# FF1 in a two-layer decoder step: eight pairs of output tiles per layer by seven block products instead of eight

## The chip, the cores and the metric

The kernel runs on one core of one Trainium2 chip. The metric is device time in microseconds (us). The profile names the engines PE (matmul), PEld (the weight loads of PE), DVE, ACT and POOL (elementwise work), and SP (a queue that issues DMAs). PE, DVE, ACT, POOL and SP each have an instruction stream of their own, taken in the order written, and meet at semaphores.

## The reference

Two layers over 512 prompt tokens and 8 sample tokens, model width 1024. What matters here is the feed-forward part, with hidden width 4096:

```python
u = x @ lp['w_in']
...                                   # attention, recurrence, pooling
mix = jnp.concatenate([attn, rec, pool], axis=-1) @ lp['w_out']
x = layer_norm(alpha * x + mix, lp['ln1_g'], lp['ln1_b'])
hid = jnp.square(jax.nn.relu(x @ lp['w_ff1']))                          # FF1: 1024 -> 4096
x = layer_norm(alpha * x + hid @ lp['w_ff2'], lp['ln2_g'], lp['ln2_b'])  # FF2: 4096 -> 1024
```

All data are float32.

## The kernel before

Activations lie transposed: 128 channels on the partitions, tokens along the free dimension, 8 such blocks for 1024 channels. Tokens come in two halves h: half 0 has 256 prompt tokens, half 1 has 256 prompt tokens and the 8 sample tokens, 264 in all (`NH`).

Each float32 operand is split into a high and a low part for PE: `xh` and `xl` for the layer's input x, `hh` and `hl` for the hidden activations, and the two planes of a weight slot. For a weight block w and an input block x three matmuls are issued: high by high, high by low, low by high. So a product of one 128-wide output tile with one token half takes 8 blocks x 3 = 24 matmuls (`product`), accumulated in one PSUM bank.

A weight tile of 128 output columns (a "unit") is split on its way: a DMA of 1 MB brings two units into one of two `raw` buffers, ACT (or POOL) casts the high plane into one of seven slots `w0` to `w6`, and DVE (or POOL) subtracts to get the low plane (`prep_to`).

The feed-forward part runs in 4 chunks p of 1024 hidden channels. For a chunk, `do_f1` makes the 8 output tiles of FF1 (ACT: relu out of PSUM into `ra`; DVE: square into `rb`; ACT: cast to `hh`; DVE: remainder to `hl`), and `do_f2` makes 8 products of FF2 whose results DVE adds to `y`. Half 0 runs chunk 0 alone, while the first layer norm of half 1 is still being computed; then both halves run chunks 1 to 3, half 0 leading by three units (`lagged`, `STEADY`); then half 1 runs chunk 0 again alone (called chunk 4), while the second norm of half 0 is computed.

The order on each engine is set at build time: every operation is recorded with its estimated duration, and a list scheduler (`Plan.order`) places them by due time. Where an operation has two possible engines (`copy`, `either`), the scheduler chooses. All instructions are issued from one line (`Plan.issue`), so the profile shows one line number for nearly everything, and one reads by tile names: `mm`, `s`, `t`, `x` are PSUM banks (3, 2, 2 and 1 of them), `acc`, `gq`, `ra`, `rb`, `rc`, `rd`, `gl` are temporaries of one token line, and `p` and `long` in the profile are wide temporaries of attention and norms.

Of the kernel before, what the change touches and what calls it, by code (L numbers as in the profile page):

```python
# [59 lines left out]
class Plan:  # L60
# [60 lines left out]
    def add(self, first, *others):  # L121

        op = Op()
        eng, method, args, kw = first
        outs = [kw[k] for k in ("out", "accum_out") if kw.get(k) is not None]
        rest = list(args)
        if "out" not in kw:
            outs.append(rest.pop(0))
        if method == "tensor_tensor_reduce":
            outs.append(rest.pop())  # L130
        ins = [a for a in rest if isinstance(a, bass.AP)]
        ins += [a for k, a in kw.items() if k not in ("out", "accum_out") and isinstance(a, bass.AP)]
        op.idx = len(self.ops)
        self.ops.append(op)
        op.alts, op.preload = {}, False
        for e, m, ar, k in others + (first,):
            op.eng, op.call = e, (getattr(self.engs[e], m), ar, k)
            self.cost(op, m, outs, ins, ar, k)
            op.alts[e] = (op.call, op.dur, op.sets, op.lock)
        deps = set()  # L140
        for a, w in [(a, False) for a in ins] + [(a, True) for a in outs]:
            nm = a.name
            if a.space == bass.MemoryType.DRAM:
                continue
            r = self.region(a)
            wl, rl = self.writes.setdefault(nm, []), self.reads.setdefault(nm, [])

            def hit(q):
                return q[0] < r[1] and r[0] < q[1] and any(x < d and c < y for x, y in q[2] for c, d in r[2])
            for q, o in wl:  # L150
                if hit(q):
                    deps.add(o)
            if w:
                for q, o in rl:
# [12 lines left out]
        deps.discard(op)  # L167
        op.deps = deps
        return op

    def cost(self, op, method, outs, ins, args, kw):
# [6 lines left out]
        op.lock = (op.eng == "G" and bool(ins) and method != "dma_start") or (op.eng == "V" and (  # L178
            len(sb) > 1 or (len(sb) == 1 and method in ("tensor_scalar", "tensor_copy"))))
        op.sets, op.bytes = None, 0  # L180
        op.side = op.eng == "T" and out.name[:2] != "mm"
        if method == "dma_start":
            b = 4
            for k in out.shape:
# [135 lines left out]
def trunk_kernel(ctx, tc, x_prompt, x_sample, cache_k, cache_v, state_h, state_conv, state_pool,  # L320
# [30 lines left out]

    def wide(name, long=False):

        return plan.tile(tmp, [128, 1056], F32, "long" if long else "p4", 1 if long else 2, name)

    def line(tag, width, name=None, parts=128, dt=F32):
        return plan.tile(tmp, [128, 288], dt, tag, 1, name or tag)[:parts, :width]

    def t_bank(shape, name="tb"):
# [85 lines left out]
    def prep_to(i):  # L445
        while nxt[0] <= min(i, len(units) - 1):
            j = nxt[0]
            nxt[0] += 1
            raw_need(j)
            key, _, view, s = units[j]  # L450
            src = view(raw_t[j], s)
# [58 lines left out]
    KZ = ctile([128, 2, 512], "KZ")  # L510
    G.memset(KZ[64:128, 0], 0.0)
    G.memset(KZ[0:64, 1], 0.0)
    onesm = ctile([128, 128], "onesm")
    G.memset(onesm, 1.0 / DM)
    epsc = ctile([128, 2], "epsc")
# [96 lines left out]


    y = {}
    xh = [act.tile([128, 8, NH[h]], F32R, tag="xh%d" % h, name="xh%d" % h) for h in range(2)]
    xl = [act.tile([128, 8, NH[h]], F32R, tag="xl%d" % h, name="xl%d" % h) for h in range(2)]
    hid = {}

    def new_hid(h):
# [2 lines left out]
    def load_x(h):  # L622
# [3 lines left out]
        for k4 in range(2):  # L626
            for t0, n, src in blocks:
# [49 lines left out]

    def layer_start(l):
        st.clear()
        load_gates(l)  # L680
# [3 lines left out]
        st["Q", 1] = plan.tile(tmp, [128, 4, NH[1]], F32, "Q1", 1, "Q1")  # L684
        st["V"] = plan.tile(tmp, [128, 4, 128], F32, "V", 1, "V")
# [6 lines left out]
        st["col"] = plan.tile(tmp, [128, 2, 43], F32, "col", 1, "colt")  # L692
# [211 lines left out]
    class Item:  # L904
# [34 lines left out]
        def turn(self):  # L939
            self.pts = []  # L940
            for b in range(self.nk // 128):
                pt = t_bank([128, 4, 128])
                for g in range(4):
                    T.transpose(pt[:, g], self.pr[:, g, b * 128:b * 128 + 128], ident)
                p = plan.tile(tmp, [128, 512], F32, "P", 4, "P")
                copy(p, pt.rearrange("p g n -> p (g n)"), "V")
                self.pts.append((b, p))

# [96 lines left out]
    class Norm:  # L1045
# [103 lines left out]
        def split(self):  # L1149
# [7 lines left out]
            for m in range(8):  # L1157
                hi, lo = xh[self.h][:, m], xl[self.h][:, m]
                z, b = self.sq[m % 2], self.col("b", m)
                V.scalar_tensor_tensor(z, yy[:, m], self.col("g", m), r, MUL, MUL)  # L1160
                if m % 2 == 0 or not MIXED:
# [112 lines left out]
    def do_f1(l, p, m, h):  # L1274
# [9 lines left out]
        S.copy(out=hi[:, m], in_=q)  # L1284
        V.tensor_tensor(lo[:, m], q, hi[:, m].bitcast(F32), SUB)

    def do_f2(l, p, m, h):
        ps = product((l, "f2%d" % p, m // 2, m % 2), h, hid[h][0], hid[h][1])
        if p == h:
            residual(h, m, ps)  # L1290
        else:
            V.tensor_tensor(y[h][:, m], y[h][:, m], ps, ADD)
        if p == 3 + h:
            norms[l, h, 2].chunk(m)

    def do_ff(l, kind, p, m, h):

        (do_f1 if kind == "f1" else do_f2)(l, p, m, h)

    def body():  # L1300
        layer_start(0)
# [3 lines left out]
        for l in range(DEPTH):  # L1305
# [67 lines left out]
                        stage(c)  # L1373
            drain()
            shift_states(l)
            both = [(kind, p, m) for p in range(1, 4) for kind in ("f1", "f2") for m in range(8)]
            ff = [((kind, 0, m), 0) for kind in ("f1", "f2") for m in range(8)]
            ff += lagged(both, STEADY, STEADY)
            ff += [((kind, 4, m), 1) for kind in ("f1", "f2") for m in range(8)]
            for (kind, p, m), h in ff:  # L1380
                prep_to(uidx[(l, "%s%d" % (kind, p), m // 2, m % 2)])
                if h == 1 and (kind, p, m) == both[0]:
                    drain()
                do_ff(l, kind, p, m, h)
                slot_end()
            drain()
# [33 lines left out]
```

## Time and profile before

| | |
|---|---|
| median of 3 runs | 1122.9 us (1122.36 to 1122.96) |
| the profiled execution's own time | 1121.61 us |
| its span | 1119.9 us |
| mean granted PE clock | 0.996 |
| DVE busy | 670.9 us |
| ACT busy | 525.4 us |
| POOL busy | 233.8 us |

The span is what the trace covers; 1.7 us of the execution's own time lie around it. The profiled execution was 1.3 us under the median. Busy shares are averages over stages with different limits, so the prediction reads the feed-forward stage by itself. A matmul's duration in the profile overlaps the next one's; the rate is read from many matmuls in a row.

### The profile page before, as it was taken

The numbers are of one execution on the slowest core, as the hardware profiler recorded it, in microseconds if no ns is written. First come the engines' busy times: TensorE is split into PE (matmuls) and PEld (weight loads), VectorE is DVE, ScalarE is ACT, GpSimd is POOL, SyncE is SP. The second block draws the span as 40 slices with busy tenths as digits, with TensorE's granted clock in tenths as the row PEclk, the third lists the DMA queues.
The fourth block names the chain that finished last, engine by engine and source line by source line (L and its number), as shares of the span: only waits on it lengthen the run. The fifth ranks groups of instructions, "written<-read, shape, count | busy, mean of one in ns | idle before, by whom it ended". The sixth has DMA issues, their size and how long they took to land.

```text
span 1119.9 us, 21316 instructions
## 1 busy us (share of the span) xinstructions
PE 1095.7 (98%) x8733; PEld 1068.8 (95%) x8733; DVE 670.9 (60%) x1369; ACT 525.4 (47%) x1036; POOL 233.8 (21%) x358
## 2 busy tenths in 40 slices
PE   7999998999999999999999999899999999999997
PEld 7988898999999999999998889899999999999996
DVE  5657678964444334469864586888444443445666
ACT  5758655544224223337476776554332332243333
POOL 4444344300000000022233453223000000002223
PEclk9999999999999999999999999999999999999999
DMA  9320313642323323234533040347223232322431
GB/s 263 113 58 18 96 43 114 209 172 76 112 78 94 95 77 113 76 104 153 159 106 97 1 114 5 114 145 232 99 83 107 76 113 76 106 84 80 147 114 40
DMA packets 120019, 116.58 MB, mean 104 GB/s; under 512 B 4480, under 2 KB 118170, under 8 KB 119874
## 3 DMA queue, kind: packets, MB, share of 16 engines
q1 hardware_dynamic: 119570, 115.16, 33.1%
q8 instruction: 68, 1.11, 0.4%
q14 instruction: 29, 0.24, 0.1%
q0 software_dynamic: 352, 0.06, 0.0%
HBM read 112.72 MB, written 4.84 MB: 105 GB/s over the span
## 4 chain that ended last, share of the span: by engine, by line
PE 88%; DVE 5%; ACT 2%; DMA 2%; issue 1%; SPq 0%; POOL 0%; DVEq 0%; ACTq 0%; POOLq 0%
PE mm L316 81%; PE t L316 3%; PE s L316 3%; PE x L316 2%; DVE y L316 1%; DMA raw<-in_w_out_dram 1%; DMA raw<-in_w_in_dram 1%; DVE w L316 1%; DVE ra L316 1%; ACT L316 1%; DVE hl L316 0%; DVE gl L316 0%; DVE rb L316 0%; DVE rd L316 0%; DVE small L316 0%
## 5 line engine op out<-in xcount | busy, mean ns | idle before, releaser
L316 PE MATMUL mm<-xh,w 128*128 128x264 f32 (+1 forms) x2816 | 537.9, 288 | 1.6 <-ACT xh L316 1.6
L316 PE MATMUL mm<-hh,w 128*128 128x264 f32 (+1 forms) x2560 | 478.9, 285 | 0.0
L316 PEld LDWEIGHTS mm<-xh,w 128*128 128x128 f32 x2816 | 443.9, 190 | 7.3 <-issue 3.8
L316 PE MATMUL mm<-xl,w 128*128 128x264 f32 (+1 forms) x1408 | 405.9, 288 | 0.0
L316 PEld LDWEIGHTS mm<-hh,w 128*128 128x128 f32 x2560 | 403.2, 190 | 0.9
L316 PE MATMUL mm<-hl,w 128*128 128x256 f32 (+1 forms) x1280 | 364.2, 285 | 0.0
L316 DVE TENSOR_TENSOR w<-raw,w 128x1024 fp32r<-128x1024 f32 (+1 forms) x195 | 243.5, 1252 | 166.1 <-ACT w L316 163.9
L316 ACT CAST w<-raw 128x1024 fp32r<-128x1024 f32 (+1 forms) x189 | 195.7, 1039 | 288.0 <-PE mm L316 252.0
L316 PEld LDWEIGHTS mm<-xl,w 128*128 128x128 f32 x1408 | 267.9, 190 | 3.9 <-issue 3.3
L316 PEld LDWEIGHTS mm<-hl,w 128*128 128x128 f32 x1280 | 243.5, 190 | 1.0 <-issue 0.3
L316 POOL TENSOR_TENSOR acc<-y 128x256 f32<-128x256 f32 (+1 forms) x8 | 7.5, 935 | 508.3 <-DVE y L316 508.3
L316 ACT CAST hh<-rb 128x264 fp32r<-128x264 f32 (+1 forms) x128 | 52.2, 410 | 107.7 <-DVE rb L316 107.6
L316 DVE TENSOR_TENSOR y<-y,mm 128x256 f32<-128x256 f32 (+1 forms) x96 | 40.6, 423 | 78.5 <-PE mm L316 78.5
L316 DVE TENSOR_TENSOR hl<-rb,hh 128x264 fp32r<-128x264 f32 (+1 forms) x128 | 54.5, 427 | 39.0 <-ACT hh L316 39.0
L316 DVE TENSOR_TENSOR rb<-ra 128x264 f32<-128x264 f32 (+1 forms) x128 | 55.4, 434 | 21.5 <-ACT ra L316 21.5
L316 ACT ACTIVATE ra<-mm 128x264 f32<-128x264 f32 (+1 forms) x128 | 48.8, 383 | 33.1 <-PE mm L316 32.8
L316 ACT ACT_TABLE_LOAD x33 | 42.3, 1283 | 3.0 <-DVE nm L316 1.7
L316 POOL TENSOR_TENSOR acc<-acc,y 128x256 f32<-128x256 f32 (+1 forms) x32 | 31.1, 972 | 50.1 <-DVE y L316 44.5
L316 POOL TENSOR_SCALAR p<-p,rs 128x256 f32<-128x256 f32 (+1 forms) x64 | 35.6, 573 | 23.2 <-DVE rs L316 13.8
L316 DVE CUSTOM_DVE_ANT_0 p<-s,delta,sink_bc 128x256 f32<-128x256 f32 (+1 forms) x64 | 26.2, 447 | 19.5 <-PE s L316 16.6
L316 ACT ACTIVATE p<-p,nm 128x257 f32<-128x257 f32 (+1 forms) x64 | 30.3, 475 | 10.5 <-DVE nm L316 10.3
L316 POOL TENSOR_SCALAR w<-raw 128x1024 fp32r<-128x1024 f32 x13 | 13.8, 1064 | 95.3 <-PE mm L316 81.8
(280 smaller groups left out, 912.2 us busy)
## 6 DMA issues: line engine op xcount, KB each, us to landing
raw<-in_w_ff_dram SPq DMA_DIRECT2D x80, 1024.0 KB
raw<-in_w_in_dram SPq DMA_DIRECT2D x7, 1024.0 KB
raw<-in_w_in_dram SPq DMA_DIRECT2D x8, 512.0 KB
raw<-in_w_out_dram SPq DMA_DIRECT2D x8, 512.0 KB
raw<-in_w_out_dram SPq DMA_DIRECT2D x16, 256.0 KB
y<-in_x_prompt_dram SPq DMA_DIRECT2D x4, 256.0 KB
raw<-in_w_in_dram SPq DMA_DIRECT2D x4, 256.0 KB
y<-in_x_prompt_dram SPq DMA_DIRECT2D x2, 512.0 KB
```

Source lines behind the costliest of these rows:

```text
L316: o.ins = fn(*args, **kw)
```

## The change

Eight times per layer two neighbouring output tiles of FF1 (256 weight columns, one `raw` buffer) and both token halves are computed together as a 2 x 2 block product. The weights are cut into four blocks: w11 and w12 are the two row halves (512 rows each) of the first tile, w21 and w22 those of the second; the tokens' blocks are the same two row halves of each token half. Seven products of half the depth (4 blocks, 12 matmuls) replace eight, in the form with nested sums known as Strassen-Winograd. The table `PAIRS` says which pairs: two in chunk 1, three each in chunks 2 and 3. The other FF1 tiles, chunk 0 and 4, and all of FF2 stay as they were.

- Once per layer `token_sums` forms four sums T1 to T4 of token blocks, 4 blocks each, and splits them into high and low planes. They lie in a new region `over`, which shares its memory with the tiles `P`, `Q1`, `V`, `KZ`, `p4`, `long`, `gl0`, `gl1` of attention and norms. `KZ` is therefore zeroed at each layer's start. `rc0`, `rc1`, `rd0`, `rd1` become one tile `four`.
- `xh` and `xl` of half 0 are made 264 wide, with zeros in the last 8 columns. The first norm of half 1 now leaves x also in `y[1]`.
- `prep_pair` forms three sums of weight blocks (four additions or subtractions of 128x512) and splits three slots and a half (a, b, c, and half of a shared d) in place of two.
- `do_pair` runs seven block products in the order p1, p5, p6, p2, p7, p3, p4, through banks `s`, `t` and `mm`, copies p1 to `gq` (e1), adds the products up on DVE in `acc` (u2, u3), and closes four tiles: add, relu and square in one DVE instruction, cast on ACT, remainder on DVE.
- Both halves finish a pair together, so the stream of FF1 and FF2 units is cut at each group of pairs: the units between groups are lagged as before, each stretch by itself.

```diff
+PAIRS = {1: (2, 3), 2: (1, 2, 3), 3: (1, 2, 3)}
...
+        t = line("rc0", 1024, "ws").rearrange("p (k c) -> p k c", k=8)
+        a = slot_for((j, "a"), 2)
+        split_w(a, r[:, :, 0:128])
+        either("V", t[:, 0:4], w21, w22, ADD)
+        either("V", t[:, 4:8], t[:, 0:4], w11, SUB)
+        either("V", w21, w11, w21, SUB)
+        b = slot_for((j, "b"), 2)
+        split_w(b, t)
+        c = slot_for((j, "c"), 2)
+        split_w(c, r[:, :, 128:256])
+        either("V", t[:, 0:4], w12, t[:, 4:8], SUB)
...
+        d = wt_t[dk]
+        split_w(d, t[:, 0:4], i % 2 * 4)
...
+    def block(ps, w, k0, x, x0, n, start, stop):
+        for k in range(4):
+            rh, rl = (a[:, x0 + k, :n] for a in x)
+            T.matmul(ps[:, :n], w[:, 0, k0 + k], rh, start=start and k == 0, stop=False)
+            T.matmul(ps[:, :n], w[:, 0, k0 + k], rl, start=False, stop=False)
+            T.matmul(ps[:, :n], w[:, 1, k0 + k], rh, start=False, stop=stop and k == 3)
...
+    def token_sums():
+        for k in range(4):
+            b1, b2 = y[1][:, k], y[1][:, 4 + k]
+            a1, a2 = ([x[:, j + k, :n].bitcast(F32) for x in xf] for j, n in ((0, 264), (4, 256)))
+            t1, t2, t3, t4 = (line(t, 264, t) for t in ("rc0", "rc1", "rd0", "rd1"))
+            t4 = t4[:, :256]
+            either("V", t3, b2, b1, SUB)
+            either("V", t1, b1, a1[0], SUB)
+            either("V", t1, t1, a1[1], SUB)
+            either("V", t2, b2, t1, SUB)
+            either("V", t4, a2[0], t2[:, :256], SUB)
+            either("V", t4, t4, a2[1], ADD)
+            for nm, t in (("T1", t1), ("T2", t2), ("T3", t3), ("T4", t4)):
+                hi, lo = (a[:, k] for a in sums[nm])
+                copy(hi, t, "V")
+                either("V", lo, t, hi.bitcast(F32), SUB)
...
+        def close(h, mm, i, a, ps):
+            n = NH[h]
+            t, q = line("ra%d" % i, n, "fr"), line("rb%d" % i, n, "fq")
+            V.tensor_tensor(t, a[:, :n], ps[:, :n], ADD)
+            V.scalar_tensor_tensor(q, t, 0.0, t, MAX, MUL)
+            hi, lo = hid[h]
+            S.copy(out=hi[:, mm], in_=q)
+            V.tensor_tensor(lo[:, mm], q, hi[:, mm].bitcast(F32), SUB)
+        p1 = mul(0, wa, 0, xf, 0, 264, (j, "a"))
+        S.copy(out=e1, in_=p1)
+        p5 = mul(1, wb, 0, sums["T1"], 0, 264, (j, "b"))
+        p6 = mul(0, wb, 4, sums["T2"], 0, 264, (j, "b"))
+        V.tensor_tensor(u2, e1, p6, ADD)
+        p2 = mul(2, wa, 4, xf, 4, 256, (j, "a"))
+        close(0, m, 0, e1, p2)
+        p7 = mul(1, wc, 0, sums["T3"], 0, 264, (j, "c"))
+        V.tensor_tensor(u3, u2, p7, ADD)
+        close(1, m + 1, 1, u3, p5)
+        p3 = mul(2, wd, d0, (xh[1], xl[1]), 4, 264, dk)
+        t = line("ra0", 264, "fr")
+        V.tensor_tensor(t, u2, p5, ADD)
+        close(1, m, 0, t, p3)
+        p4 = mul(0, wc, 4, sums["T4"], 0, 256, (j, "c"))
+        close(0, m + 1, 1, u3, p4)
```

Where the scheduler put the new work, first DVE in layer 0 at the start of chunk 1. Before, the last additions of chunk 0 (`y`) are followed by the squares and remainders of the first FF1 tiles and one weight split now and then:

```order
L316 SCALAR_TENSOR_TENSOR y0_0_90<-xl0_115,y0_0_90 128x256
L316 TENSOR_TENSOR rb0_0_163<-ra0_0_160 128x256
L316 TENSOR_TENSOR hl0_0_128<-rb0_0_163,hh0_0_127 128x256
L316 TENSOR_TENSOR rb1_0_165<-ra1_0_161 128x256
L316 TENSOR_TENSOR hl0_0_128<-rb1_0_165,hh0_0_127 128x256
```

Now the sums T1 to T4 (`four` to `over_r`) and the sums and splits of the first pair's weights stand between them:

```order
L319 TENSOR_TENSOR four_97<-four_97,xl0_115 128x256
L319 TENSOR_TENSOR over_r_56<-four_97,over_r_56 128x264 x3
L319 TENSOR_TENSOR four_97<-raw_0_93 128x512
L319 TENSOR_TENSOR over_r_56<-four_97,over_r_56 128x256
L319 TENSOR_TENSOR w5_89<-raw_0_93,w5_89 128x1024
L319 TENSOR_TENSOR four_97<-four_97,raw_0_93 128x512
L319 TENSOR_TENSOR raw_0_93<-raw_0_93 128x4x128
L319 TENSOR_TENSOR hl0_0_125<-rb1_0_153,hh0_0_124 128x256
L319 TENSOR_TENSOR hl0_0_125<-rb0_0_152,hh0_0_124 128x256
L319 TENSOR_TENSOR w6_90<-four_97,w6_90 128x1024
```

The squares and remainders moved back behind them. The second place is DVE in chunk 2 of layer 0, where FF1's tiles 2 and 3 stood before:

```order
L316 TENSOR_TENSOR w4_86<-raw_0_91,w4_86 128x1024
L316 TENSOR_TENSOR rb1_0_165<-ra1_0_161 128x264
L316 TENSOR_TENSOR hl1_0_130<-rb1_0_165,hh1_0_129 128x264
L316 TENSOR_TENSOR rb0_0_163<-ra0_0_160 128x256
L316 TENSOR_TENSOR hl0_0_128<-rb0_0_163,hh0_0_127 128x256
L316 TENSOR_TENSOR w5_87<-raw_0_91,w5_87 128x1024
```

Now the first pair of that chunk is added up and closed there (`acc_0` is u2, `acc_1` is u3, `gq` is e1), and the third pair's sum of weights (`four` from `raw_1`) stands ahead of it:

```order
L319 TENSOR_TENSOR four_97<-four_97,raw_1_95 128x512
L319 TENSOR_TENSOR acc_0_156<-gq_0_117,s_0_143 128x264
L319 TENSOR_TENSOR ra0_0_150<-gq_0_117,mm_1_129 128x256
L319 TENSOR_TENSOR acc_1_157<-acc_0_156,t_0_122 128x264
L319 TENSOR_TENSOR ra1_0_151<-acc_1_157,t_1_123 128x264
L319 SCALAR_TENSOR_TENSOR rb0_0_152<-ra0_0_150 128x256
L319 SCALAR_TENSOR_TENSOR rb1_0_153<-ra1_0_151 128x264
L319 TENSOR_TENSOR ra0_0_150<-acc_0_156,t_1_123 128x264
L319 TENSOR_TENSOR ra0_0_150<-ra0_0_150,mm_2_130 128x264
L319 TENSOR_TENSOR ra1_0_151<-acc_1_157,s_1_144 128x256
```

The weight splits of the pair moved ahead of its products, into the FF2 stretch of the chunk before, and DVE now reads PSUM itself where ACT's relu did.

More of the change, by code (lines that the diff above doesn't have):

```diff
@@ L70, in __init__ @@
         self.rings, self.psum = {}, set()
+        self.alias, self.large = {}, False
     def tile(self, pool, shape, dt, tag, bufs, name, psum=False):
@@ L141, in add @@
         for a, w in [(a, False) for a in ins] + [(a, True) for a in outs]:
-            nm = a.name
+            nm = self.alias.get(a.name, a.name)
             if a.space == bass.MemoryType.DRAM:
@@ L180, in cost @@
         op.sets, op.bytes = None, 0
-        op.side = op.eng == "T" and out.name[:2] != "mm"
+        op.side = op.eng == "T" and not self.large and out.name[:2] != "mm"
         if method == "dma_start":
@@ L337, in either, with turn @@
         return plan.add(*((e, "tensor_tensor", (out, a, b, op), {}) for e in (first, {"V": "G", "G": "V"}[first])))
+    at, n_over = 195808, 8384
+    nc.alloc_sbuf_tensor("over", [128, n_over], F32, side="right")
+    over_f = nc.alloc_sbuf_tensor_at("over_f", [128, n_over], F32, offset=at).ap()
+    over_r = nc.alloc_sbuf_tensor_at("over_r", [128, n_over], F32R, offset=at).ap()
+    plan.alias[over_r.name] = over_f.name
+    place = {}
+    for nm, n in (("P", 2048), ("Q1", 1056), ("V", 512), ("KZ", 1024), ("p4", 2112), ("long", 1056), ("gl0", 288), ("gl1", 288)):
+        o = sum(x.shape[1] for x in place.values())
+        place[nm] = over_f[:, o:o + n]
+    turn_of = {"p4": 0, "P": 0}
+    def turn(nm, n, k):
+        i = turn_of[nm] % k
+        turn_of[nm] += 1
+        return place[nm][:, i * n:i * n + n]
     const = ctx.enter_context(tc.tile_pool(name="const", bufs=1))
@@ L352, in wide @@
     def wide(name, long=False):
-        return plan.tile(tmp, [128, 1056], F32, "long" if long else "p4", 1 if long else 2, name)
+        return place["long"] if long else turn("p4", 1056, 2)
+    four = {}
     def line(tag, width, name=None, parts=128, dt=F32):
+        if tag in ("gl0", "gl1"):
+            return place[tag][:parts, :width]
+        if tag in ("rc0", "rc1", "rd0", "rd1"):
+            if not four:
+                four[0] = tmp.tile([128, 4 * 288], F32, name="four", tag="four")
+            i = ("rc0", "rc1", "rd0", "rd1").index(tag) * 288
+            return four[0][:parts, i:i + width]
         return plan.tile(tmp, [128, 288], dt, tag, 1, name or tag)[:parts, :width]
@@ L436, in trunk_kernel, with slot_for, slot_used, is_pair @@
     raw_t = {}
+    def slot_for(key, uses):
+        i = min((i for i in range(NW) if all(i != v[0] for v in live.values())), key=lambda i: used[i])
+        live[key] = [i, uses]
+        return slots[i]
+    def slot_used(key):
+        used[live[key][0]] = len(plan.ops)
+        live[key][1] -= 1
+        if not live[key][1]:
+            del live[key]
+    def is_pair(j):
+        key = units[j][0]
+        return key[1][:2] == "f1" and key[2] in PAIRS.get(int(key[1][2]), ())
+    def split_w(w, src, k0=0):
+        n = src.shape[1]
+        hi, lo = w[:, 0, k0:k0 + n], w[:, 1, k0:k0 + n]
+        copy(hi, src, "G")
+        either("V", lo, src, hi.bitcast(F32), SUB)
+    def prep_pair(j):
+        key = units[j][0]
+        r = raw_t[j]
+        w11, w12 = r[:, 0:4, 0:128], r[:, 4:8, 0:128]
+        w21, w22 = r[:, 0:4, 128:256], r[:, 4:8, 128:256]
+        t = line("rc0", 1024, "ws").rearrange("p (k c) -> p k c", k=8)
[9 more added lines that the diff above has]
+        either("V", t[:, 0:4], w12, t[:, 4:8], SUB)
+        group = PAIRS[int(key[1][2])]
+        i = group.index(key[2])
+        dk = key[:2] + (i // 2,)
+        if i % 2 == 0:
+            wt_t[dk] = slot_for(dk, min(2, len(group) - i))
+        d = wt_t[dk]
+        split_w(d, t[:, 0:4], i % 2 * 4)
+        wt_t[j] = (a, b, c, d, i % 2 * 4, dk)
     nxt = [0]
@@ L450, in prep_to @@
             key, _, view, s = units[j]
+            if is_pair(j):
+                if s == 0:
+                    prep_pair(j)
+                continue
             src = view(raw_t[j], s)
@@ L509, in trunk_kernel @@
     G.tensor_scalar(sink_bc, sink_bc, -1.0, 1.0, MUL, MUL)
-    KZ = ctile([128, 2, 512], "KZ")
-    G.memset(KZ[64:128, 0], 0.0)
-    G.memset(KZ[0:64, 1], 0.0)
+    KZ = place["KZ"].rearrange("p (v n) -> p v n", v=2)
     onesm = ctile([128, 128], "onesm")
@@ L614, in trunk_kernel @@
     y = {}
-    xh = [act.tile([128, 8, NH[h]], F32R, tag="xh%d" % h, name="xh%d" % h) for h in range(2)]
-    xl = [act.tile([128, 8, NH[h]], F32R, tag="xl%d" % h, name="xl%d" % h) for h in range(2)]
+    xh = [act.tile([128, 8, 264], F32R, tag="xh%d" % h, name="xh%d" % h) for h in range(2)]
+    xl = [act.tile([128, 8, 264], F32R, tag="xl%d" % h, name="xl%d" % h) for h in range(2)]
+    zero = line("gq", 64, "zero")
+    V.memset(zero, 0.0)
+    for x in (xh, xl):
+        S.copy(out=x[0][:, :, 256:264], in_=zero.rearrange("p (k n) -> p k n", k=8))
+    xf = (xh[0], xl[0])
+    xh[0], xl[0] = xh[0][:, :, :256], xl[0][:, :, :256]
     hid = {}
@@ L635, in load_x @@
                 yield 1
+    def block(ps, w, k0, x, x0, n, start, stop):
+        plan.large = True
+        for k in range(4):
[3 more added lines that the diff above has]
+            T.matmul(ps[:, :n], w[:, 1, k0 + k], rh, start=False, stop=stop and k == 3)
+        plan.large = False
     def product(key, h, rh, rl, mid=None, add=()):
@@ L679, in layer_start @@
         st.clear()
+        G.memset(KZ[64:128, 0], 0.0)
+        G.memset(KZ[0:64, 1], 0.0)
         load_gates(l)
@@ L683, in layer_start @@
         st["Q", 0] = y_slot(0, "Q0")[:, 1088:2112].rearrange("p (g n) -> p g n", g=4)
-        st["Q", 1] = plan.tile(tmp, [128, 4, NH[1]], F32, "Q1", 1, "Q1")
-        st["V"] = plan.tile(tmp, [128, 4, 128], F32, "V", 1, "V")
+        st["Q", 1] = place["Q1"].rearrange("p (g n) -> p g n", g=4)
+        st["V"] = place["V"].rearrange("p (b n) -> p b n", b=4)
         r0 = y_slot(1, "r0")
@@ L691, in layer_start @@
         st["hlast"] = plan.tile(tmp, [128, 2], F32, "hlast", 1, "hlast")
[L692 removed]
+        st["col"] = r0[:, 2020:2106].rearrange("p (c n) -> p c n", c=2)
         sl = wide("state", True)
@@ L944, in turn @@
                     T.transpose(pt[:, g], self.pr[:, g, b * 128:b * 128 + 128], ident)
-                p = plan.tile(tmp, [128, 512], F32, "P", 4, "P")
+                p = turn("P", 512, 4)
                 copy(p, pt.rearrange("p g n -> p (g n)"), "V")
@@ L1160, in split @@
                 V.scalar_tensor_tensor(z, yy[:, m], self.col("g", m), r, MUL, MUL)
-                if m % 2 == 0 or not MIXED:
+                if PAIRS and self.h == 1 and self.which == 1:
+                    S.activation(out=yy[:, m], in_=z, func=AF.Identity, bias=b)
+                    copy(hi, yy[:, m], "V")
+                    either("V" if m % 2 else "G", lo, yy[:, m], hi.bitcast(F32), SUB)
+                elif m % 2 == 0 or not MIXED:
                     S.activation(out=hi, in_=z, func=AF.Identity, bias=b)
@@ L1285, in do_f1 @@
         V.tensor_tensor(lo[:, m], q, hi[:, m].bitcast(F32), SUB)
+    sums = {}
+    o = 0
+    for nm, n in (("T1", 264), ("T2", 264), ("T3", 264), ("T4", 256)):
+        sums[nm] = []
+        for _ in range(2):
+            sums[nm].append(over_r[:, o:o + 4 * n].rearrange("p (k n) -> p k n", k=4))
+            o += 4 * n
+    def token_sums():
[14 more added lines that the diff above has]
+                either("V", lo, t, hi.bitcast(F32), SUB)
@@ new lines, in do_pair, with bank, mul @@
+    def do_pair(l, p, c):
+        m = 2 * c
+        if m == 0:
+            new_hid(0), new_hid(1)
+        j = uidx[(l, "f1%d" % p, c, 0)]
+        prep_to(j + 1)
+        wa, wb, wc, wd, d0, dk = wt_t[j]
+        e1 = line("gq", 264, "e1")
+        u2, u3 = (plan.tile(tmp, [128, 264], F32, "acc", 2, "acc") for _ in range(2))
+        def bank(k):
+            pool, tag, bufs = ((ps_s, "s", 2), (ps_t, "t", 2), (ps_mm, "mm", 3))[k]
+            return plan.tile(pool, [128, 264], F32, tag, bufs, tag, True)
+        def mul(k, w, k0, x, x0, n, key=None):
+            ps = bank(k)
+            block(ps, w, k0, x, x0, n, True, True)
+            if key:
+                slot_used(key)
+            return ps
+        def close(h, mm, i, a, ps):
[22 more added lines that the diff above has]
+        close(0, m + 1, 1, u3, p4)
@@ L1296, in do_ff @@
     def do_ff(l, kind, p, m, h):
-        (do_f1 if kind == "f1" else do_f2)(l, p, m, h)
+        if kind == "pair":
+            do_pair(l, p, m)
+        else:
+            (do_f1 if kind == "f1" else do_f2)(l, p, m, h)
     def body():
@@ L1375, in body @@
             shift_states(l)
-            both = [(kind, p, m) for p in range(1, 4) for kind in ("f1", "f2") for m in range(8)]
             ff = [((kind, 0, m), 0) for kind in ("f1", "f2") for m in range(8)]
+            both = []
+            for p in range(1, 4):
+                group = PAIRS.get(p, ())
+                both += [("f1", p, m) for m in range(8) if m // 2 not in group]
+                if group:
+                    ff += lagged(both, STEADY, STEADY)
+                    ff += [(("pair", p, c), 0) for c in group]
+                    both = []
+                both += [("f2", p, m) for m in range(8)]
             ff += lagged(both, STEADY, STEADY)
+            if PAIRS:
+                token_sums()
             ff += [((kind, 4, m), 1) for kind in ("f1", "f2") for m in range(8)]
+            drained = False
             for (kind, p, m), h in ff:
-                prep_to(uidx[(l, "%s%d" % (kind, p), m // 2, m % 2)])
-                if h == 1 and (kind, p, m) == both[0]:
+                if kind != "pair":
+                    prep_to(uidx[(l, "%s%d" % (kind, p), m // 2, m % 2)])
+                if h == 1 and not drained:
                     drain()
+                    drained = True
                 do_ff(l, kind, p, m, h)
```

## The prediction

> **What bounds the kernel now.** I read the page's head first, then the stages, then the chain of waits. The head gives span and busy times; its fourth part gives the engines on the chain that ended last.
>
> ```profile
> span 1119.9 us, 21316 instructions
> PE 1095.7 (98%) x8733; PEld 1068.8 (95%) x8733; DVE 670.9 (60%) x1369; ACT 525.4 (47%) x1036; POOL 233.8 (21%) x358
> PE 88%; DVE 5%; ACT 2%; DMA 2%; issue 1%; SPq 0%; POOL 0%; DVEq 0%; ACTq 0%; POOLq 0%
> ```
>
> PE is busy 98% of the span and makes 88% of the chain. Matmuls overlap in this view, so busy alone does not say that fewer matmuls take less time. The stages of layer 0's feed-forward part say more (busy us of each engine, PE clock, DMA share, GB/s):
>
> ```profile
> core 0: us, PE busy (x) PEld busy (x) DVE busy (x) ACT busy (x) POOL busy (x), PEclk, DMA share, GB/s
> 193.00:204.00 11.00, 11.00 (x94) 11.00 (x93) 10.90 (x22) 8.00 (x18) 1.14 (x1) 1.00 0.44 150
> 204.00:216.00 12.00, 12.00 (x103) 12.00 (x102) 10.91 (x19) 8.05 (x16) 3.48 (x2) 1.00 0.66 216
> 216.00:239.00 23.00, 23.00 (x194) 23.00 (x193) 19.64 (x33) 10.77 (x17) 7.25 (x6) 1.00 0.67 220
> 239.00:262.00 23.00, 23.00 (x194) 23.00 (x193) 9.78 (x19) 9.45 (x20) 0.00 (x0) 1.00 0.32 107
> 285.00:331.00 46.00, 46.00 (x385) 46.00 (x384) 21.46 (x36) 10.52 (x14) 0.00 (x0) 1.00 0.30 93
> ```
>
> From 193 to 239 (chunk 0, half 0 alone, while half 1's norm runs) PE is full though DVE is busy 85 to 99%. From 239 on (chunks 1 to 3, both halves) PE is full and DVE below half. The chain of waits, asked for three parts of that layer (start, length, what), holds matmuls alone:
>
> ```profile
> 203.88 34.20 PE mm L316 x285
> 239.88 230.19 PE mm L316 x1916
> 503.19 43.72 PE mm L316 x360
> ```
>
> The first is half 0 alone: 34.20 / 285 = 0.1200 us a matmul of 256 columns. The second has both halves: 230.19 / 1916 = 0.1201. The third is half 1 alone, 264 columns: 0.1214. So a matmul costs 0.120 us, nearly whatever its width, and in chunks 1 to 3 the time is the number of matmuls.
>
> **The change, part by part.** *Matmuls removed.* A pair took 4 products of 24 = 96 matmuls; it takes 7 of 12 = 84. With 8 pairs in each of 2 layers that is 12 x 16 = 192 matmuls fewer, all in the stretch of the second chain row: 192 x 0.1201 = 23.1 us. Columns do not enter this: the 84 have 60 of width 264 and 24 of 256, and by the first two rows that is under 0.3 us in all.
>
> [...]
>
> *DVE work added.* Durations by shape, then DVE and POOL in order of time (start, length, what), to see what of a duration is overlap:
>
> ```profile
> L316 DVE TENSOR_TENSOR w<-raw,w 128x1024 fp32r<-128x1024 f32 x191 | 240.7, 1263 | 164.4 <-ACT w L316 162.2 <-PE t L316 1.0
> L316 DVE TENSOR_TENSOR w<-raw,w 128x512 fp32r<-128x512 f32 x4 | 2.8, 693 | 1.7 <-ACT w L316 1.7
> L316 DVE TENSOR_TENSOR rb<-ra 128x264 f32<-128x264 f32 x64 | 28.7, 448 | 3.0 <-ACT ra L316 3.0
> 203.46 1.22 DVE L316 TENSOR_TENSOR w<-raw,w 128x1024 fp32r<-128x1024 f32 x1
> 204.59 0.42 DVE L316 TENSOR_TENSOR rb<-ra 128x256 f32<-128x256 f32 x1
> 232.34 1.76 DVE L316 SCALAR_TENSOR_TENSOR y<-xl,y 128x256 f32<-128x256 f32 x5
> 212.94 1.63 DVE L316 TENSOR_TENSOR w<-raw,w 128x1024 fp32r<-128x1024 f32 x1
> 213.58 3.26 POOL L316 TENSOR_TENSOR w<-raw,w 128x1024 fp32r<-128x1024 f32 x1
> ```
>
> A split of 1.22 us is followed 1.13 later by the next instruction, and five small ones take 1.76, so (1.76 - 0.42) / 4 = 0.34 each: the last 0.08 of each overlaps. In a queue a split therefore costs 1.13, one of 512 columns 0.693 - 0.08 = 0.61, a small one 0.34. The last two rows show a split beside one on POOL: 1.63 instead of 1.22.
>
> A pair then asks DVE for 15 additions and closings x 0.34 = 5.1, three and a half splits, 3 x 1.13 + 0.61 = 4.0, and four sums of 512 columns, 2.4: together 11.5 us. Before, the four products and two splits asked 8 x 0.34 + 2 x 1.13 = 5.0. PE needs 84 x 0.120 = 10.1 for a pair. So DVE alone would be slower than PE, by 1.4 us a pair, if all of it stood inside the pair and POOL took nothing. It does not stand there: by the order, the first two pairs of a group are split during the FF2 units before it, where DVE is below half busy, and in the first two pairs of chunk 2 DVE's queue between one u2 and the next holds 15 and 16 instructions, one and two of them splits: 14 x 0.34 + 1.13 = 5.9 and 14 x 0.34 + 2 x 1.13 = 7.0 us, of 10.1. Over chunk 2 DVE has 3 x 11.5 for the pairs, 5.0 for the two tiles left, and for FF2 8 splits and 16 additions, 14.5: 54 us, in 32 x 24 x 0.1201 - 3 x 1.44 = 88 us of PE, less what POOL takes.
>
> Price of the pairs' waits: PSUM banks come free late if DVE is late, and PE stands behind them. Bounds: nothing (by the row at 204: DVE 10.91 of 12 busy, PE 12.00 of 12), and 1.4 x 16 = 22 us with no head start and no help. Below nothing is excluded, since PE has no wait there to lose. I take 0.15 a pair, 2.4 us, near the lower end, because the row at 204 is the nearest: DVE as full as in the densest pair, with the same shapes.
>
> *The token sums.* 24 additions and 16 remainders a layer, 40 x 0.34 = 13.6 us of DVE, and 16 casts on ACT. By the order they stand between the last FF2 eviction of chunk 0 and the first pair. From that eviction to u2 of the first pair DVE's queue holds 1 + 58 instructions: 6 splits, 8 of 512 columns, 45 small ones: 6.8 + 4.9 + 15.3 = 27.0 us. PE has there 8 FF1 products and three of the pair's, 8 x 24 + 36 = 228 matmuls, 27.4 us. So DVE arrives at u2 with nothing to spare, and POOL holds some five of the sums and splits at the same place, by this row:
>
> ```profile
> L316 POOL TENSOR_TENSOR w<-raw,w 128x1024 fp32r<-128x1024 f32 x7 | 18.4, 2635 | 2.0 <-ACT w L316 1.8
> ```
>
> Two of 1024 columns, two of 512 (half of it each) and one small one of about 1 us make 8.9 us of POOL. Behind u2 stand 6 more DVE instructions until bank `t` is free, 2.4 us with u2, and PE asks for that bank 5 products, 7.2 us, after u2's data: 4.8 us of slack. If DVE lost all of POOL's 8.9 us it would be 8.5 late and PE would wait 3.7; if it lost 0.41 for each split (1.63 against 1.22), nothing. Between 0 and 3.7 a layer I take 0.5, near the row with both engines: 1.0 us in all.
>
> *ACT.* Casts, and one PSUM copy for four relus:
>
> ```profile
> L316 ACT CAST w<-raw 128x1024 fp32r<-128x1024 f32 x185 | 193.3, 1048 | 281.2 <-PE mm L316 252.0 <-DMA raw<-in_w_ff_dram 15.7 <-DMA raw<-in_w_out_dram 8.8
> L316 ACT CAST hh<-rb 128x264 fp32r<-128x264 f32 x64 | 26.4, 412 | 75.9 <-DVE rb L316 75.9
> ```
>
> 3.5 x 1.05 + 4 x 0.41 + 0.4 = 5.7 us of 10.1 a pair; PE hides it, nothing taken. If DVE were late, the casts would be late with it, which is in the price above.
>
> *Loads.* SP issues the same 1 MB per pair, now every 10.1 us instead of 11.5, into the same two buffers, each kept until the pair's last split. The row at 216 shows 220 GB/s moved with PE full; a pair asks 104. Nothing taken; a late pair split would delay the load of the FF2 units queued behind it on SP.
>
> *Start of a layer, and the rest.* Two more zeroings of `KZ`, 0.52 us each on POOL by the next row, stand in POOL's queue ahead of two weight splits of FF2; the zero columns and the altered norm (a cast more for four blocks) lie under chunk 0's matmuls or the first loads. Between 0 and 1.0; I take 0.2.
>
> ```profile
> L316 POOL MEMSET KZ<- 64x512 f32 x2 | 1.0, 520 | 0.1
> ```
>
> *From the last pair to FF2.* Both halves now end together: after p4 DVE has 7 small instructions and a cast lies between, about 3.3 us, and by the order PE does 40 matmuls, 4.8 us, before it needs the last remainder. Hidden; without that reordering it would cost 0.8 (the last block is needed 2.5 us after p4) in each of 6 groups, which I leave in the range.
>
> **Sum.** -23.1 + 2.4 + 1.0 + 0.2 = -19.5. The profiled execution took 1121.61 (span 1119.9 and 1.7 around it): 1102.1. The median of the runs is 1.3 higher, so 1103.4.
>
> **The rivals.**
>
> DVE sets part of the pace. For it: 11.5 us a pair against 10.1, a queue in order whose remainders wait for ACT's casts, and zero slack at the first pair. Against it: the row at 204. At half the upper bound, 11 of 22 us, and the 3.7 a layer: 1122.9 - 23.1 + 11 + 7.4 = 1118; at a quarter, 1110. With the whole bound it ends at no change.
>
> DVE and POOL block each other, the side that ends slower. The order gives POOL 34 splits and 24 operations of 512 columns more, 34 x 2.64 + 24 x 1.32 = 121 us, 7.6 a pair, and leaves DVE 11.5 - (34 x 1.13 + 24 x 0.61) / 16 = 8.2. If the two never ran at once and half of POOL's fell inside the pairs, a pair took 8.2 + 3.8 = 12.0 us against 11.53 before: 0.5 x 16 = 8 us slower, 1131. It decides from 3.3 us of POOL in a pair on. Against it: at 213 DVE's split ended within POOL's, 0.41 longer, so they did not exclude each other for POOL's 3.26. [...]
>
> The change does not save what it says: the 192 matmuls go, but PE waits where they were, for a weight slot. Seven slots hold two pairs exactly. Against it, the third pair's first slot is free 4.4 us into the first pair, 15 us before it is needed, and cast and POOL split take 1.05 + 2.64. It is the no-change end of the first rival.
>
> **Chances.** Forecast, pairs nearly hidden, 1099 to 1107: 0.72. DVE sets part of the pace, 1107 to 1120: 0.18, about half of it to 1112. No change: 0.03. Slower by the port: 0.06. Still faster than the whole 23.1: 0.01. Low end: all 23.1 saved on the profiled time, 1098.5. High end 1112, which leaves out some 0.18. Within 0.2% (2.2 us) is about what a measurement of this kernel cannot tell from no change; by the same cases faster has 0.91, same 0.03, slower 0.06.
>
> **What would show it.** Right: 192 matmuls fewer on PE; chain rows of chunks 1 to 3 that still hold matmuls alone, at 0.120 each; DVE near full only from chunk 0 to the first pair; PE idle under 0.5 us inside a group. Wrong: PE waiting for DVE at bank `s` or `t` (for `acc` or `ra`) in every pair, or for `over_r` at p5 of the first pair; DVE splits well over 1.3 us on average, with POOL busy beside them; weight loads of PE waiting for `w`.

## The result and the profile after

The changed kernel takes 1117.4 us (median of 4 runs, 1116.54 to 1118.36) against 1122.9 before: a ratio of 0.995 (95% interval 0.9933 to 0.9968). It is faster by 5.5 us where 19.5 were forecast, and lies above the forecast range. The profiled execution took 1118.36 us. The head of its page shows that the matmuls went as counted, 8733 - 8541 = 192, and that PE's busy time fell by 12.9 us only:

```profile
span 1116.6 us, 21329 instructions
PE 1082.8 (97%) x8541; PEld 1051.9 (94%) x8541; DVE 800.6 (72%) x1598; ACT 544.1 (49%) x1055; POOL 366.4 (33%) x428
```

The stages of layer 0 (columns as before) show where PE is no longer full. Up to 262, where the token sums stand, it is; at 274, in and behind chunk 1's second pair, 2.16 us are missing, and then the granted clock falls:

```profile
239.00:262.00 23.00, 23.00 (x194) 23.00 (x193) 22.80 (x49) 13.80 (x30) 0.93 (x1) 1.00 0.16 53
262.00:274.00 12.00, 11.83 (x98) 11.62 (x97) 8.78 (x16) 6.37 (x11) 10.23 (x5) 1.00 0.48 153
274.00:285.00 11.00, 8.84 (x70) 8.63 (x69) 10.32 (x14) 3.07 (x6) 8.06 (x4) 0.95 0.52 161
285.00:297.00 12.00, 12.00 (x93) 12.00 (x92) 6.05 (x16) 2.69 (x4) 2.40 (x1) 0.90 0.16 53
366.00:377.00 11.00, 10.18 (x85) 9.97 (x84) 10.58 (x18) 4.66 (x8) 5.00 (x2) 1.00 0.56 180
```

PE's list of waits (what PE was about to write, what released it: us in total, times, longest) has new entries for `hh` and `hl`, which FF2 reads behind the last pair of a group. The waits inside the pairs, at banks `s` and `t`, are small:

```profile
PE mm L319 <- DVE y L319: 4.6, 2, 2.4
PE mm L319 <- ACT hh L319: 4.4, 2, 2.2
PE mm L319 <- DVE hl L319: 3.1, 4, 0.8
PE t L319 <- DVE ra L319: 0.8, 4, 0.2
PE s L319 <- DVE ra L319: 0.3, 2, 0.2
```

The timeline at the end of chunk 1 (start, length, what) shows how a wait of 2.17 us comes about:

```profile
272.14 9.92 POOL L319 TENSOR_TENSOR w<-raw,w 128x1024 fp32r<-128x1024 f32 x4 [1.76 <-ACT w L319]
...
274.91 4.92 DVE L319 TENSOR_TENSOR hl<-rb,hh 128x256 fp32r<-128x256 f32 x2
279.75 0.42 DVE L319 TENSOR_TENSOR acc<-acc,t 128x264 f32<-128x264 f32 x1
280.20 0.43 DVE L319 TENSOR_TENSOR ra<-acc,t 128x264 f32<-128x264 f32 x1
280.67 2.02 DVE L319 SCALAR_TENSOR_TENSOR rb<-ra 128x264 f32<-128x264 f32 x2
...
282.38 0.74 ACT L319 CAST hh<-rb 128x264 fp32r<-128x264 f32 x2 [3.91 <-DVE rb L319]
...
280.73 0.28 PE L319 MATMUL mm<-hh,w 128*128 128x256 f32 x1
283.18 0.50 PE L319 MATMUL mm<-hh,w 128*128 128x256 f32 x2 [2.17 <-ACT hh L319]
```

POOL runs four weight splits back to back from 272.14 to 282.06, about 2.5 us each. Beside them two remainders take DVE 4.92 us instead of 0.76, and the next square about 1.7 instead of 0.42. The two additions between them, which read one operand from PSUM (`t`), take 0.42 as ever. The groups of the whole execution say the same (mean ns of one; `hl` had 430 before):

```profile
L319 DVE TENSOR_TENSOR hl<-rb,hh 128x264 fp32r<-128x264 f32 x64 | 53.2, 832 | 1.9 <-ACT hh L319 1.9
L319 DVE SCALAR_TENSOR_TENSOR rb<-ra 128x264 f32<-128x264 f32 x32 | 27.7, 864 | 0.5
L319 DVE TENSOR_TENSOR ra<-acc,t 128x264 f32<-128x264 f32 x32 | 13.6, 424 | 0.5
```

The second loss is the clock. Three stretches of the changed kernel, the granted clock in the third column from the right:

```profile
181.50:188.30 6.80, 5.95 (x27) 5.95 (x28) 5.66 (x12) 2.54 (x8) 4.53 (x4) 0.50 0.21 74
188.40:192.00 3.60, 3.60 (x33) 3.60 (x32) 2.12 (x4) 1.67 (x4) 1.98 (x2) 1.00 0.92 291
283.90:287.30 3.40, 3.40 (x19) 3.40 (x18) 2.63 (x8) 1.76 (x3) 0.32 (x1) 0.51 0.82 269
```

19 matmuls touch the last of them, of 3.40 us, where 33 touch the 3.60 us at full clock. The stretch at 283.9 follows the wait above; the one at 181.5 follows PE's wait for `y` before the last out-projection product, which stood there before too. Both come again in layer 1. The kernel before had one such stretch of 3.4 us with products in it, in layer 1.

The account of the profiled executions: the spans differ by 3.3 us, 19.8 less than the 23.1 of the matmuls. PE's new waits in the feed-forward parts (each a distance between two matmul starts, less 0.12) make 5.2 in layer 0 and 5.4 in layer 1: six of 0.3 to 0.4 inside the groups, four of 0.8 to 1.0 behind those of chunks 2 and 3, two of 2.3 behind those of chunk 1. Ahead of the last norm, half clock takes 20.4 us against 3.4; a matmul then takes 0.22 us instead of 0.12, so 17.0 more cost some 7 (0.85 and 1.1 us in them were waits). The wait for `y` is longer by 0.7 in all. Together 18 of the 19.8; what the other 1.5 or so are was not found.

### The profile page after: what moved, and what is told of

It reads as the page before. It is cut to its first block, busy times and chain, and to the rows that moved or that the text cites. A ratio compares the mean times of both kernels' runs of the same rounds, so it can differ in the third digit from the quotient of the medians.

```text
span 1116.6 us, 21329 instructions
## 1 busy us (share of the span) xinstructions
PE 1082.8 (97%) x8541; PEld 1051.9 (94%) x8541; DVE 800.6 (72%) x1598; ACT 544.1 (49%) x1055; POOL 366.4 (33%) x428
## 5 line engine op out<-in xcount | busy, mean ns | idle before, releaser
L319 PE MATMUL mm<-xh,w 128*128 128x264 f32 (+1 forms) x2048 | 400.8, 289 | 1.1 <-ACT xh L319 1.0
L319 PEld LDWEIGHTS mm<-xh,w 128*128 128x128 f32 x2048 | 324.1, 189 | 7.1 <-issue 3.8
L319 PE MATMUL mm<-xl,w 128*128 128x264 f32 (+1 forms) x1024 | 295.9, 289 | 0.0
L319 PEld LDWEIGHTS mm<-xl,w 128*128 128x128 f32 x1024 | 193.4, 189 | 4.0 <-issue 3.4
L319 POOL TENSOR_TENSOR w<-raw,w 128x1024 fp32r<-128x1024 f32 x37 | 95.0, 2574 | 53.3 <-ACT w L319 53.1
L319 PE MATMUL t<-over_r,w 128*128 128x264 f32 x384 | 52.2, 285 | 0.8 <-DVE ra L319 0.8
L319 PE MATMUL s<-over_r,w 128*128 128x264 f32 (+1 forms) x384 | 51.5, 283 | 0.3 <-DVE ra L319 0.3
L319 PEld LDWEIGHTS t<-over_r,w 128*128 128x128 f32 x384 | 48.7, 188 | 1.7 <-DVE ra L319 1.7
L319 PEld LDWEIGHTS s<-over_r,w 128*128 128x128 f32 x384 | 48.2, 188 | 0.9 <-DVE ra L319 0.8
L319 DVE SCALAR_TENSOR_TENSOR rb<-ra 128x256 f32<-128x256 f32 (+1 forms) x64 | 45.6, 737 | 0.6
```

The costliest lines, as they stand in the source:

```text
L319: o.ins = fn(*args, **kw)
```

## The experiments

Two theories stood against each other: DVE is late because POOL's splits hold it up (theory 1), or because its own queue is too long (theory 2). A third question was whether the clock follows from the waits. All ratios are to the kernel before on the same chip; the changed kernel's is 0.995.

**POOL out of the weights of chunks 1 to 3.**

```diff
-        copy(hi, src, "G")
-        either("V", lo, src, hi.bitcast(F32), SUB)
+        copy(hi, src, "")
+        V.tensor_tensor(lo, src, hi.bitcast(F32), SUB)
...                       # the four sums of prep_pair and prep_to's splits likewise
```

> POOL takes no part in the weights of chunks 1 to 3: all casts there on ACT, all sums and low planes on DVE (about 34 splits and 24 sums of 512 columns more for DVE, 34 x 1.13 + 24 x 0.61 = 53 us). Theory 1, DVE is late because POOL's back-to-back splits hold up its instructions with two operands in SBUF: squares and remainders of the pairs go back to 0.42 us each, the wait of 2.2 us behind chunk 1's last pair falls under 0.9, the half clock behind it goes, and the time is 1108 to 1112. Theory 2, DVE's own queue is too long and POOL was a help: the waits in and behind the pairs grow, and the time is 1120 or more.

Measured 1102.5 us, ratio 0.9805 (0.979 to 0.9821): theory 1, with more gained than it expected. Between the two profiled executions, 15.9 us apart, the waits of the feed-forward parts went from 10.6 to 0.8 us, and half clock ahead of the last norm from 20.4 to 6.8, which makes some 6 more. DVE has 58 instructions more and is busy 791.5 us instead of 800.6. Two of its stages and two of its groups:

```profile
259.00:271.00 12.00, 12.00 (x102) 12.00 (x101) 12.00 (x23) 7.10 (x13) 0.00 (x0) 1.00 0.26 88
271.00:282.00 11.00, 11.00 (x94) 11.00 (x93) 11.00 (x26) 5.37 (x8) 0.00 (x0) 1.00 0.58 193
```

```profile
L319 DVE TENSOR_TENSOR hl<-rb,hh 128x264 fp32r<-128x264 f32 x64 | 27.1, 424 | 1.9 <-ACT hh L319 1.9
L319 DVE SCALAR_TENSOR_TENSOR rb<-ra 128x264 f32<-128x264 f32 x32 | 13.2, 423 | 0.0
```

DVE is busy without a gap, POOL not at all, and PE is full. A full queue alone does not make PE wait here. One wait of 0.8 us is left in all the groups of the two layers, and there PE waits for POOL's zeroing of `KZ` for the next layer (`over_f` in the list of waits), not for DVE. The half clock of 283.9 is gone (clock 1.00 from 274 to 297), and that behind the wait for `y` is 3.4 us long in each layer.

**POOL's splits in smaller pieces.** The order on every engine is that of the changed kernel; each low plane of 1024 columns on POOL is issued as four instructions.

```diff
+                if o.eng == "G" and len(o.alts) > 1 and len(args) == 4 and tuple(args[0].shape) == (128, 8, 128):
+                    for k in range(0, 8, 2):
+                        o.ins = fn(*(a[:, k:k + 2] for a in args[:3]), args[3])
+                    continue
```

> The changed kernel with the same order, but each low plane of 1024 columns that POOL computes is issued as four instructions of 256. If a DVE instruction with both operands in SBUF is held up until the POOL instruction in progress ends, its longest duration falls from 2.6 us to about 1.1 (0.42 + 0.65), the wait of 2.2 behind chunk 1's last pair to about 0.5, and the time to 1105 to 1110. If POOL holds the port for as long as it has work, or slows DVE by taking a share, durations and time stay: 2.6 us and 1117, or more by POOL's three more starts a split.

Measured 1110.5 us, ratio 0.9879 (0.9863 to 0.9896): 7 us less by the medians, 8 by the ratios, with the same POOL work in the same order.

```profile
L323 DVE TENSOR_TENSOR hl<-rb,hh 128x264 fp32r<-128x264 f32 x64 | 42.9, 670 | 2.4 <-ACT hh L323 2.4
L323 DVE SCALAR_TENSOR_TENSOR rb<-ra 128x256 f32<-128x256 f32 x32 | 25.3, 790 | 0.1
L321 POOL TENSOR_TENSOR w<-raw,w 128x256 fp32r<-128x256 f32 x148 | 123.9, 868 | 30.0 <-ACT w L323 29.8
```

The longest square or remainder of the pairs fell from 2.63 to 1.53 us, not quite to the 1.1 expected; more of them are held up (`rb` of 256 columns has a mean of 790 instead of 610), each by less. POOL pays as well: 868 ns a piece, where a quarter of its 2574 would be 644. The wait behind chunk 1's last pair fell to 1.2 us in layer 0 and 1.6 in layer 1, where 0.5 was expected, and no half clock follows it any more (mean granted clock 0.991 against 0.986). The waits of the feed-forward parts make 6.9 us instead of 10.6, so about half of the gain is theirs; the rest fits the clock, with 13.7 us at half clock ahead of the last norm instead of 20.4. So what holds DVE up ends with a POOL instruction, not with POOL's run of work: 1.53 us at most beside pieces of 868 ns, 2.63 beside splits of 2574. What the two engines share, which the forecast above and the prediction's chances call the port, no run shows.

**Pairs ahead of the ordinary tiles in chunks 2 and 3.**

```diff
-PAIRS = {1: (2, 3), 2: (1, 2, 3), 3: (1, 2, 3)}
+PAIRS = {1: (2, 3), 2: (0, 1, 2), 3: (0, 1, 2)}
...
+                    both = [("f1", p, m) for m in range(8) if m // 2 > group[-1]]
```

> In chunks 2 and 3 the three pairs come first (column groups 0 to 2) and the ordinary tiles 6 and 7 stand between the last pair and FF2; chunk 1 as it was. If PE waits behind the last pair because FF2 needs its remainders too soon, the four waits of 0.8 to 1.0 us go (4.0 us in all): 1113 to 1114. If DVE is late for other reasons, the wait turns up inside the pairs and the time stays at 1117.

Measured 1112.2 us, ratio 0.989 (0.9872 to 0.9908). The four waits of 0.8 to 1.0 are gone but for 0.6 us in chunk 2 of each layer; chunk 1's two, of 2.2, stay. The gain on the changed kernel, 6.7 us by the ratios, is more than the 4.0 of the waits. In the profile the half clock behind the wait for `y` has 3.4 us in place of 6.8, and layer 1 has none behind chunk 1's pairs although the wait is as long (mean granted clock of the profiled execution 0.992 against 0.986): part of the gain is the clock's.

With POOL out as well:

> POOL out of the weights of chunks 1 to 3, and the pairs of chunks 2 and 3 ahead of the ordinary tiles. If POOL's splits were the only reason for the waits behind the pairs, the new place adds nothing: 1101 to 1103. If FF2 asked too soon on top of it, 1099 to 1101.

Measured 1100.7, ratio 0.98 (0.9786 to 0.9815), against 0.9805 for POOL out alone: the two intervals nearly coincide. The place of the pairs matters as long as DVE is held up, and hardly otherwise. A gain of 1 or 2 us could be hidden here: the profiled execution has 6.8 us of half clock behind the wait for `y` in each layer, where POOL out alone has 3.4.

**Filling the waits.** The first try gave 18 unread matmuls to each wait, with their duration known to the scheduler.

```diff
...
+            op = T.matmul(ps, w[:, 0, k % 8], xh[h][:, k % 8], start=True, stop=True)
...
```

> 18 matmuls into a bank that nobody reads (2.2 us at full clock) are put into the wait behind chunk 1's last pair and 18 into the wait before the last out-projection product, in each layer: 72 matmuls of work that is not wanted, 8.6 us if nothing hid them. Theory 1, a wait of over 2 us halves the PE clock for 3.4 or 6.8 us, which costs 1.5 us for each 3.4: the half-clock periods behind both places go, and the time falls by 5 to 8 us, to 1109 to 1112. Theory 2, the halving doesn't come from the wait: the periods stay, and the time is 1117 or, with the matmuls' own time, up to 1126.

Measured 1135.2 us, ratio 1.0098 (1.0082 to 1.0115), which tells nothing of the clock: with PE 2 us later in its plan, the scheduler gave POOL other work. Two whole splits back to back now stood beside the first pair, where half a split and a whole one had stood, and PE waited there:

```profile
265.48 5.06 POOL L319 TENSOR_TENSOR w<-raw,w 128x1024 fp32r<-128x1024 f32 x2
...
271.33 0.78 PE L319 MATMUL t<-over_r,w 128*128 128x264 f32 x2 [2.98 <-DVE ra L319]
```

That 8.6 us of work made it some 17 us slower shows how much hangs on where a POOL split stands. The second try planned the same matmuls at no duration (and took data that no engine was writing), which left the order of all engines as it was:

```diff
...
+            op = T.matmul(ps, w[:, 0, k % 8], rhs[:, k % 8], start=True, stop=True)
+            op.dur = 0.0
...
```

> The changed kernel with the same order on every engine, and 18 matmuls that nobody reads in each of the two waits per layer (behind chunk 1's last pair; before the last out-projection product), planned at no duration so that nothing else moves. If a wait of over 2 us halves the clock, the half-clock periods of 3.4 us (283.9, 826.7) and of 6.8 us (181.5, 724.3) go while the waits become work: 4 to 8 us off the changed kernel, 1109 to 1113. If the matmuls are only added work, 72 x 0.12 less the waits' 9 us: 1117 to 1118, and the periods stay.

Measured 1110.5 us, ratio 0.9885 (0.9871 to 0.99). Two stages and the filled wait:

```profile
178.00:200.00 22.00, 21.80 (x175) 21.42 (x176) 19.42 (x34) 12.97 (x30) 9.70 (x8) 1.00 0.41 136
285.00:297.00 12.00, 12.00 (x102) 12.00 (x101) 7.25 (x15) 2.10 (x2) 0.51 (x1) 1.00 0.29 87
```

```profile
276.95 2.31 PE L319 MATMUL x<-xh,w 128*128 128x256 f32 x18
279.30 0.50 PE L319 MATMUL mm<-hh,w 128*128 128x256 f32 x2
```

The needed products waited as long, but PE was busy, and the clock stayed full until the last norm, at 1097.8. So the halving follows from the wait, and costs the changed kernel some 7 us.

Not all of this was the change's. The same matmuls before the last out-projection product, alone, in the changed kernel with POOL out and in the kernel before:

> POOL out of the weights of chunks 1 to 3, and 18 matmuls that nobody reads in the wait before the last out-projection product, planned at no duration. If the half clock of 3.4 us behind that wait comes from the wait, it goes in both layers: 2 x 1.5 = 3 us under POOL out alone, 1099 to 1101. If not: 1102.5, or up to 1 us more.

Measured 1100.4, ratio 0.9796 (0.9781 to 0.981): 2.1 us under POOL out alone by the medians, 1.0 by the ratios, whose intervals overlap; the half clock there is gone (mean granted clock 0.997 against 0.994).

> The kernel before, with the same 18 matmuls in the wait before the last out-projection product. The trace of before has one half-clock period of 3.4 us there in one of the layers: if the matmuls take it away, 1121 to 1122, and little of what they gave the changed kernel was to be had before. If they give as much as in the changed kernel with POOL out (2 us or more), the wait's clock is no part of what the change cost.

Measured 1120.2, ratio 0.9974 (0.9963 to 0.9984): 2.8 us were to be had without the change, no less than with it and POOL out. So some 4 of the 7 can be charged to the change; both figures are known to about 2 us only.

**No pairs at all.**

```diff
-PAIRS = {1: (2, 3), 2: (1, 2, 3), 3: (1, 2, 3)}
+PAIRS = {}
```

> No pairs at all, and no token sums and no altered norm; the new places of the temporaries in memory, the zeroing of KZ in each layer and the zero columns stay. If these cost nothing, the time is that of the kernel before, 1122 to 1124, and the changed kernel owes all its 5.5 us to the pairs; if the longer wait and the half clock before the last out-projection product come from them, it is 1126 to 1128 with 6.8 us of half clock there in each layer.

Measured 1126.2 us, ratio 1.0022 (1.0011 to 1.0034). The new places in memory and the rest cost about 2.5 us by the ratio. The median lies in the second case, 1126 to 1128; the ratio puts the time between the two cases. Its stage around the wait for `y`:

```profile
178.00:200.00 22.00, 16.69 (x115) 15.97 (x113) 14.94 (x26) 8.49 (x19) 8.18 (x7) 0.84 0.42 138
```

Half clock lasts 6.8 us behind that wait in both layers, and layer 0's wait is longer, the order there having moved. Which of the changed places moved it was not tried.

**All three edits together.**

> POOL out of the weights of chunks 1 to 3, pairs of chunks 2 and 3 ahead of the ordinary tiles, and 18 matmuls that nobody reads in the wait before the last out-projection product. If the three are independent (1.8 us from the new place and 2.1 from the matmuls, on 1102.5): 1098 to 1099. If the new place's gain was the clock's phase alone: 1100.

Measured 1098.1 us, ratio 0.978 (0.9764 to 0.9796): 2.2% under the kernel before. It is the fastest version that was run, and the time is that of three independent gains. By the ratios the new place gives 1.8 us here, on 0.9796 without it, but the two intervals overlap.

## Why the prediction was wrong

*What bounds the kernel, and the matmuls.* Right: 192 matmuls fewer, and with POOL out 21.9 us of time (1.95% of 1122.9), near the forecast's 19.5.

*The pairs' waits, 2.4.* Inside the groups PE waits 0.3 to 0.4 us once per group, 2.2 us in all. The size came out right by luck: DVE is not merely full, as in the row at 204, but held up, and with POOL out these waits are gone though DVE is full.

*The token sums, 1.0.* PE is full from 239 to 262, with DVE at 22.80 of 23: near 0 there.

*From the last pair to FF2, nothing.* This is the term that failed. It priced 7 small instructions and a cast at 3.3 us, every small one at 0.34. Beside POOL they cost up to 2.6 each, and behind the six groups PE waits 8.4 us in all, which are gone with POOL out.

*DVE and POOL block each other.* The step behind that term: "at 213 DVE's split ended within POOL's, 0.41 longer, so they did not exclude each other". In those two rows DVE had begun first (212.94 against 213.58), and it was POOL that took 3.26 us instead of 2.6. DVE's 0.41 belongs to another POOL instruction, a cast that was under way when DVE's split came. It ended at 213.49, and the split 1.08 us behind it:

```profile
212.43 1.06 POOL L316 TENSOR_SCALAR w<-raw 128x1024 fp32r<-128x1024 f32 x1 [18.00 <-PE mm L316]
```

Here the one that comes second waits, on either side, so these rows spoke for the blocking and were read against it. Near its end the trace of before shows it at greater length. There POOL holds a split, and DVE comes:

```profile
1051.68 2.38 POOL L316 TENSOR_TENSOR w<-raw,w 128x1024 fp32r<-128x1024 f32 x1 [0.40 <-ACT w L316]
1051.83 2.25 DVE L316 SCALAR_TENSOR_TENSOR small<-small 128x2 f32<-128x2 f32 x1 [0.27 <-ACT small L316]
...
1088.28 2.41 POOL L316 TENSOR_TENSOR w<-raw,w 128x1024 fp32r<-128x1024 f32 x1
1088.66 3.11 DVE L316 TENSOR_TENSOR w<-raw,w 128x1024 fp32r<-128x1024 f32 x1
```

An instruction on two columns, 0.15 us elsewhere, takes 2.25, until POOL's split has ended; and DVE's split of 1088.66 ends 1.08 us behind POOL's, as the one of 212.94 did behind the cast. In the changed kernel it goes with where DVE reads: `hl`, with both operands in SBUF, took 832 ns of DVE on average, and 424 with POOL out; `ra`, with one operand in PSUM, took 424, and 0.43 us at 280.20, beside POOL. The rival had the blocking and a wrong price: it let POOL hold up all of a pair, and it forecast 1131. Squares and remainders pay most. Their four groups (`hl` and the pairs' `rb`, of 264 and 256 columns) cost DVE 130.7 us against 79.8 with POOL out, 51 us; some 11 more lie in the third of the weights' sums (1327 ns instead of 682) and in the splits. By the prediction's prices POOL's 34 splits and 24 sums spared DVE 53. So the harm is at least as large as the help: with POOL out DVE is busy 9 us less. And the harm falls on the instructions that PE waits for. The prediction's own sign of this, DVE splits well over 1.3 us on average, could not show it: they have 1.275, since it is the short instructions that are held up.

*DVE sets part of the pace.* This rival's 1118, at half of its bound, is near the measured 1117.4 by luck. It laid 11 us of waits inside the pairs and 7.4 on the token sums, where 2.2 and about 0 were found, and gave DVE's own length as the reason, which the runs without POOL rule out.

*The rest, 0.2.* About 2.5 us, by the kernel without pairs, whose profile points to a place that the prediction did not look at: the wait for `y`. Which of the changed places costs it stays open.

*The clock.* No term of the sum. Behind a wait of 2.2 us, half clock adds 1.5 us for each 3.4 us of it, some 7 in the profiled execution.

That execution took 1118.36 us where 1102.1 was forecast, 16.3 more. The waits behind the groups make 8.4 of it, the clock some 7, the longer wait for `y` 0.7; the other terms, 3.6 in the forecast, came to about 2.2.

## What to carry to other kernels

When work is given to a second elementwise engine, look in the trace for a pair of rows in which that engine began first and the other came second, and price every short instruction with two operands in SBUF at the whole length of what it may meet: here 0.42 us became up to 2.63 beside splits of 2574 ns. A helper that costs as much as it takes over is worth nothing, and less when the delay falls on the path: either keep it off that stretch (1102.5 us here against 1117.4), or cut its instructions short (1110.5). Ask of every new wait on PE of some 2 us what it does to the clock behind it: here 2.17 us were followed by 3.4 us at 0.51.

## What the runs showed of the hardware

A wait of 2.17 us on PE was enough to halve the granted clock (0.51 from 283.9 to 287.3); with unread matmuls in that wait it stayed at 1.00. In the changed kernel the half-clock stretches begin at 181.5, 283.9, 724.3 and 826.7 and last 6.8, 3.4, 6.8 and 3.4 us. The second begins 102.4 us behind the first, which is 30 times 3.413; the last two lie 159.0 and 189.0 times 3.413 us behind the first. So, by the author's estimate, they fit a grid that runs on by itself, with a period of 102.4 / 30 us, worked out from these starts and the length of 3.4, and it depends on where a wait falls in it: in the kernel before, PE's waits of 1.97 us before the last out-projection product were followed by a half-clock stretch in layer 1 (0.50 from 726.1 to 729.5) and by none in layer 0 (1.00 from 181.5 to 188.3). Counted on the grid at 0.12 us a matmul, with the shorter waits beside it, layer 1's left 3.0 us without a matmul in one stretch of 3.413, layer 0's 1.9 and 1.6 in two neighbouring ones. The waits of 0.8 to 1.0 behind the pairs of chunks 2 and 3 were never followed by one (1.00 from 287.3 to 724.2, and from 830.1 to 1106).
